# Norm chains of the second block kept apart by token half, with the first half's products ahead

## The chip, the core and the metric

The kernel runs on one core of a Trainium2 chip. TensorE (PE) multiplies; VectorE (DVE), ScalarE (ACT) and GpSimd (POOL) do the element-wise work; SyncE (SP) issues the weight loads. The metric is the time of one execution on the device in microseconds (us), taken as the median of several runs of one kernel.

## What is computed

Two blocks of a network work on 256 tokens of width 2048. The change lies in the second block, after its two output projections:

```python
x = x + rms_norm(o @ w_out[i], ln_mix_post[i])
h = rms_norm(x, ln_ffn_pre[i])
g, u = jnp.split(h @ w_gate_up[i], 2, axis=-1)
f = (jax.nn.silu(g) * u) @ w_down[i]
x = x + rms_norm(f, ln_ffn_post[i])
gate = jax.nn.sigmoid(rms_norm(x, ln_pli[i]) @ w_pli_gate[i])
x = x + gate * (p[i] @ w_pli_proj[i])
```

`rms_norm` divides each token's row of 2048 features by its root mean square, so the factor of a token is known only when the last column of its projection is there.

## The kernel before, in words

**Matrices.** Every fp32 product is made of three products of rounded parts: an operand is split into `hi` and `lo`, and hi·hi, hi·lo and lo·hi are added up in PSUM. Weights arrive as 256x512 pieces (`load`, line 354); each is split by ACT (`whi`, line 325) and DVE (`wlo`, line 326) into one of three ring buffers (`split`). `Block.steps` issues a unit of two k-tiles (k counts the 16 slices of 128 features) and all its matmuls stand on line 383. A unit of the projections (mode "tm") walks the two halves of the tokens, t = 0 and t = 1, and within each half its two k-tiles.

**Projections.** `project` (lines 1175 to 1200) runs the columns in groups (0, 1), (2), (3) of 512. When a group ends, ACT squares its PSUM tiles with a running sum (line 1188), DVE copies them to SBUF tiles `F[t, n]` (line 1205), and after group 2 the sums of the first three are put into `part`. Group 3's sum and copies are left to `post_norm`.

**The norm.** `post_norm` (lines 1207 to 1243) adds the last sum for both halves (1210), takes the power -1/2 on POOL (226), and builds for each half a diagonal matrix `dg` of its factors on ACT (1218). For k < 4 (`lead`) a product with `dg` on PE (1228, an fp32 matmul that the trace shows as two passes) scales and transposes in one; from k = 4 on, ACT scales `F` in place (1233) and PE transposes it (1234, one pass). For every k both halves land side by side in one PSUM buffer of the pool `pss`, which has three such buffers of 512 columns, one bank each; only 256 columns are used. DVE then adds the result to the residual `xr[k]` (1237), ACT and DVE split the scaled residual into `H[k]` (991, 992). After k = 5, 7, 9 and so on, one unit of the block that follows (`first`) is issued, four k-tiles behind. In the second norm, `x_rows` (1298, 1299) adds four transposes behind each unit.

**What follows.** `x_stats` squares the 16 tiles `xr` on ACT (929) and adds them up on DVE (930), while PE does two units of the block `second`; then PE needs the sum (`tok_sums`, line 240).

**Order.** PE's order is that of the program. The other engines are ordered by a scheduler at build time; `hot()` raises an operation over the weight splits. The order of every engine is then fixed, and each runs its queue in order.

Of the kernel before, what the change touches and what calls it, by code (L numbers as in the profile page):

```python
# [13 lines left out]
AF = mybir.ActivationFunctionType  # L14
ALU = mybir.AluOpType
# [4 lines left out]
P = 128  # L20
D = 2048
KT = D // P
L = 256
# [147 lines left out]
def kernel(ctx: ExitStack, tc: tile.TileContext, x, cx, vec, w_mod, w_in, ret_decay_f, ret_decay_b,  # L171
                           w_out, p_2, w_in_2, w_out_2, rel_bias, w_gate_up, w_down, w_pli_gate, w_pli_proj,
                           kca, kcr, kcb, out):
    nc = tc.nc
    out = out[0]
# [3 lines left out]
    def mk(pool, shape, tag, dt=F32, bufs=None):  # L179
        uid[0] += 1  # L180
        return pool.tile(shape, dt, tag=tag, name=f"{tag}_{uid[0]}", bufs=bufs)
# [15 lines left out]
    def side_ps():  # L197
        return mk(pss, [P, 512], "sd")
# [8 lines left out]
    def C(name, rows=P):  # L207
        a, b = CA[name]
        return ca[:rows, a:b]

    ident, ones = C("ident"), C("ones")
    V = {}
    for g, rows in enumerate(VEC_ROWS):
        o = g * P
# [5 lines left out]
    def hot():  # L220
        return tc.high_priority(offset=HOT)

    def rsq(v, n, tag="rq"):
        r = mk(sm, [P, n], tag)
        with hot():
            nc.gpsimd.tensor_tensor(out=r, in0=v, in1=C("nhalf")[:, :n], op=ALU.pow)
        return r

    def mean_eps(ps, n, width):
        v = mk(sm, [P, n], "mv")  # L230
        with hot():
            nc.vector.tensor_scalar(out=v, in0=ps, scalar1=1.0 / width, scalar2=EPS, op0=ALU.mult, op1=ALU.add)
        return v

    def tok_sums(accs):

        ps = side_ps()
        for a, acc in enumerate(accs):
            for t in range(2):
                nc.tensor.matmul(ps[:, 2 * a + t:2 * a + t + 1], lhsT=acc[:, t * P:(t + 1) * P],  # L240
                                 rhs=ones[:, 0:1], start=True, stop=True)
        return ps[:, :2 * len(accs)]
# [67 lines left out]
    for i in range(WB):  # L310
        for part in ("whi", "wlo"):
            mk(wsp, [P, 1024 + STEP // 4], f"{part}{i}", F32R)
            n = small.pop(0)
# [15 lines left out]
    class Block:  # L329
# [65 lines left out]
        def unit(self, kk):  # L395
            for _ in self.steps(kk):
                pass

        def run(self, korder):
            for a in range(0, len(korder), 2):  # L400
                self.unit(korder[a:a + 2])
            return self.ps
# [18 lines left out]
    xr = [None] * KT  # L421
# [4 lines left out]
    for s, src in enumerate((x, cx)):  # L426
        for a in range(2):
# [3 lines left out]
            for b in (0, 4):  # L431
                tc.keep_in_program_order(nc.sync.dma_start(out=xi[:, b:b + 4, :],
                                                           in_=src[:, 8 * a + b:8 * a + b + 4, :]))
# [530 lines left out]
    with hot():  # L964
        r = rsq(mean_eps(tok_sums(sqa), 4, D), 4)
# [22 lines left out]
    def scaled_split(dst, src, col):  # L988

        hi, lo = dst[:2]  # L990
        nc.scalar.activation(out=hi, in_=src, func=AF.Copy, scale=col)
        nc.vector.scalar_tensor_tensor(out=lo, in0=src, scalar=col, in1=hi, op0=ALU.mult, op1=ALU.subtract)

    def hl(pool, tag):
        return pair(pool, L, tag)
# [3 lines left out]
    ss8 = mk(hp, [P, 2, 4], "ss8")  # L999
    part = mk(hp, [P, 2], "part")  # L1000
# [154 lines left out]
    for g in range(2):  # L1155
        for kind, c0 in ((stick, 0), (dilated, 3072)):
# [10 lines left out]
            ps = Block(w_in_2, [(c0 + 2048 + 512 * g, 512)], mov, L, "tm", KT).run(ks)[0]  # L1167
# [5 lines left out]
    F = {}  # L1173

    def project(w, mov, korder, split_at):

        late = []
        for cbs in ((0, 1), (2,), (3,)):
            b = Block(w, [(cb_ * 512, 512) for cb_ in cbs], mov, L, "tm", len(korder))
            for a in range(0, len(korder), 2):  # L1180
                if cbs[0] == 0 and a == split_at:
                    sideq.drain()
                b.unit(korder[a:a + 2])
            for ci, cb_ in enumerate(cbs):
                for t in range(2):
                    jk = mk(tb, [P, 512], "tmp", BF16)
                    with hot():
                        nc.scalar.activation(out=jk, in_=b.ps[ci][t], func=AF.Square,
                                             accum_out=ss8[:, t, cb_:cb_ + 1])
                    for c_ in range(2):  # L1190
                        n = 2 * cb_ + c_
                        F[t, n] = mk(rp, [P, L], f"b{8 * t + n}")
                        late.append((F[t, n], b.ps[ci][t][:, c_ * L:(c_ + 1) * L]))
            if cbs[0] < 3:
                copies(late)
                late = []
            if cbs[0] == 2:
                nc.vector.tensor_reduce(out=part, in_=ss8[:, :, :3], axis=AX.X, op=ALU.add)
                nc.vector.tensor_scalar(out=part, in0=part, scalar1=1.0 / D, scalar2=EPS, op0=ALU.mult, op1=ALU.add)
        return late  # L1200

    def copies(todo):
        for f, ps in todo:
            with hot():
                nc.vector.tensor_copy(out=f, in_=ps)

    def post_norm(late, gain, next_gain, first, also=None):

        with hot():
            nc.vector.scalar_tensor_tensor(out=part, in0=ss8[:, :, 3], scalar=1.0 / D, in1=part, op0=ALU.mult,  # L1210
                                           op1=ALU.add)
        r = rsq(part, 2)
        copies(late)
        dg = []
        for t in range(2):
            d = mk(sm, [P, P], "dg")
            with hot():
                nc.scalar.activation(out=d, in_=ident, func=AF.Copy, scale=r[:, t:t + 1])
            dg.append(d)
        lead = 4  # L1220
        for k in range(KT + lead):
            if k < KT:
                ps = side_ps()
                for t in range(2):
                    f = F[t, k // 2]
                    o = (k % 2) * P
                    if k < lead:
                        nc.tensor.matmul(ps[:, t * P:(t + 1) * P], lhsT=f[:, o:o + P], rhs=dg[t],
                                         start=True, stop=True)
                        continue  # L1230
                    if k % 2 == 0:
                        with hot():
                            nc.scalar.activation(out=f, in_=f, func=AF.Copy, scale=r[:, t:t + 1])
                    nc.tensor.transpose(ps[:, t * P:(t + 1) * P], f[:, o:o + P], ident)  # L1234
                H[k] = hl(hp, f"h{k}")
                with hot():
                    nc.vector.scalar_tensor_tensor(out=xr[k], in0=ps[:, :L], scalar=V[gain][:, k:k + 1], in1=xr[k],
                                                   op0=ALU.mult, op1=ALU.add)
                    scaled_split(H[k], xr[k], V[next_gain][:, k:k + 1])
            if k % 2 and k > lead:  # L1240
                first.unit([k - lead - 1, k - lead])
                if also is not None:
                    also(k - lead - 1)

    def x_stats(b):

        for k in range(KT):
            sq_acc(xr[k], sqa[0], k == 0)
        b.run(ks[:4])
        m = mean_eps(tok_sums(sqa[:1]), 2, D)  # L1250
        b.run(ks[4:8])
        return rsq(m, 2)

    sideq.cap, sideq.rate = 4, 2
    late = project(w_out_2, lambda k: O[k], [0, 1, 2, 3, 8, 9, 10, 11, 4, 5, 6, 7, 12, 13, 14, 15], 12)
    def gate(j):
        return Block(w_gate_up, [(j * 512, 512)], mov, L, "fm", KT)

    def up(j):
        return Block(w_gate_up, [(DFF + j * 512, 512)], mov, L, "fm", KT)  # L1260

    first = gate(0)
    post_norm(late, "lpost", "lfpre", first)
    second = up(0)
    r = x_stats(second)
# [7 lines left out]
    for j in range(FT // 4):  # L1273
# [5 lines left out]
        ps = (second.ps if j == 0 else up(j).run(ks))[0]  # L1279
        for n in range(4):  # L1280
            f = 4 * j + n
            nc.vector.tensor_tensor(out=sgt[n], in0=ps[n][:, :L], in1=sgt[n], op=ALU.mult)
            nc.scalar.copy(out=G[f][0], in_=sgt[n])
            nc.vector.tensor_tensor(out=G[f][1], in0=sgt[n], in1=G[f][0], op=ALU.subtract)
    late = project(w_down, lambda k: G[k], list(range(FT)), -1)
    p4.close()
    p5 = ExitStack()
# [12 lines left out]

    first = Block(w_pli_gate, [(0, 512)], mov, L, "tm", KT)
    post_norm(late, "lfpost", "lpli", first, x_rows)
    second = Block(w_pli_gate, [(512, 512)], mov, L, "tm", KT)
    rp2 = x_stats(second)
# [47 lines left out]
```

## Time and profile before

| what | value |
|---|---|
| median of three runs | 2828.59 us (2826.74 to 2828.80) |
| the profiled execution, its time | 2829.03 us |
| span of the profiled execution | 2827.3 us |
| first norm, last projection matmul to first gate matmul | 1983.31 to 1989.44 us |
| second norm, the same | 2721.77 to 2727.44 us |

The profile is one execution. In its rows a group of instructions is given by start, duration, engine, line, tiles written and read, and in square brackets the idle time before it and what ended that time. "PE" rows are matmuls, "PEld" rows weight loads of TensorE.

### The profile page before, as it was taken

The numbers are of one execution on the slowest core, as the hardware profiler recorded it, in microseconds if no ns is written. First come the engines' busy times: TensorE is split into PE (matmuls) and PEld (weight loads), VectorE is DVE, ScalarE is ACT, GpSimd is POOL, SyncE is SP. The second block draws the span as 40 slices with busy tenths as digits, with TensorE's granted clock in tenths as the row PEclk, the third lists the DMA queues.
The fourth block names the chain that finished last, engine by engine and source line by source line (L and its number), as shares of the span: only waits on it lengthen the run. The fifth ranks groups of instructions, "written<-read, shape, count | busy, mean of one in ns | idle before, by whom it ended". The sixth has DMA issues, their size and how long they took to land.

```text
span 2827.3 us, 37469 instructions
## 1 busy us (share of the span) xinstructions
PE 2790.4 (99%) x14206; PEld 2345.9 (83%) x14206; DVE 1765.9 (62%) x2948; ACT 1227.4 (43%) x1964; POOL 82.6 (3%) x133
## 2 busy tenths in 40 slices
PE   7999999999999999999999999999999999999999
PEld 3588888888888878888888888888888888888878
DVE  4456765767586674745777765665766666654465
ACT  3323322422242253533556555554644544444464
POOL 0000000000000000100000010000000000000000
PEclk9999999999999999999999999999999999999999
DMA  9864454444465544646666665556556666666655
GB/s 370 299 181 137 141 164 153 145 146 143 163 207 168 169 156 156 210 142 185 210 201 214 200 202 171 165 167 191 163 188 193 188 192 188 192 193 193 208 177 168
DMA packets 159670, 522.80 MB, mean 185 GB/s; under 512 B 18232, under 2 KB 36928, under 8 KB 159232
## 3 DMA queue, kind: packets, MB, share of 16 engines
q1 hardware_dynamic: 155296, 508.78, 56.4%
q0 software_dynamic: 2752, 9.19, 1.2%
q8 instruction: 111, 1.82, 0.3%
q10 hardware_dynamic: 1440, 2.43, 0.2%
q14 instruction: 71, 0.58, 0.1%
HBM read 509.83 MB, written 7.88 MB: 183 GB/s over the span
## 4 chain that ended last, share of the span: by engine, by line
PE 96%; DMA 2%; DVE 1%; issue 0%; ACT 0%; SPq 0%; POOL 0%; DVEq 0%; ACTq 0%; POOLq 0%
PE mm L383 89%; PE sd L520 1%; DMA raw<-in_w_mod_dram 1%; PE sd L643 1%; PE sd L630 1%; PE sd L637 0%; PE sd L621 0%; DVE wlo L326 0%; PE sd L496 0%; PE sd L383 0%; DMA v<-in_ctx_dram 0%; DMA big<-in_w_mod_dram 0%; PE sd L1234 0%; PE sd L670 0%; DVE macc L489 0%
## 5 line engine op out<-in xcount | busy, mean ns | idle before, releaser
L326 DVE TENSOR_TENSOR wlo<-raw,whi 128x1024 fp32r<-128x1024 f32 (+1 forms) x764 | 916.3, 1200 | 796.7 <-ACT whi L325 794.1
L325 ACT CAST whi<-raw 128x1024 fp32r<-128x1024 f32 (+1 forms) x764 | 787.0, 1031 | 1289.9 <-PE mm L383 976.8
L383 PE MATMUL mm<-a,whi 128*128 128x512 f32 x3488 | 1134.7, 395 | 3.2 <-ACT a L558 1.6
L383 PEld LDWEIGHTS mm<-a,whi 128*128 128x128 f32 x3488 | 650.2, 188 | 160.4 <-issue 19.3
L383 PE MATMUL mm<-a,wlo 128*128 128x512 f32 (+1 forms) x2256 | 770.0, 341 | 0.0
L383 PE MATMUL mm<-h,whi 128*128 128x512 f32 x1920 | 670.9, 392 | 0.0
L383 PE MATMUL mm<-h,wlo 128*128 128x256 f32 x1920 | 541.2, 282 | 0.0
L383 PEld LDWEIGHTS mm<-a,wlo 128*128 128x128 f32 x2256 | 425.3, 189 | 49.6
L383 PEld LDWEIGHTS mm<-h,whi 128*128 128x128 f32 x1920 | 360.5, 188 | 75.2 <-issue 0.6
L383 PEld LDWEIGHTS mm<-h,wlo 128*128 128x128 f32 x1920 | 363.2, 189 | 0.0
L489 DVE SCALAR_TENSOR_TENSOR macc<-raw,s,macc 128x512 f32<-128x512 f32 x420 | 292.7, 744 | 59.8 <-DMA raw<-in_w_mod_dram 58.8
L383 PE MATMUL mm<-whi,f 128*128 128x512 f32 x704 | 216.8, 389 | 0.0
L383 PE MATMUL mm<-whi,h 128*128 128x512 f32 (+1 forms) x576 | 172.1, 373 | 0.0
L383 PE MATMUL mm<-whi,a 128*128 128x512 f32 x512 | 158.9, 390 | 0.0
L383 PEld LDWEIGHTS mm<-whi,f 128*128 128x128 f32 x704 | 132.1, 188 | 27.3
L383 PE MATMUL mm<-wlo,f 128*128 128x512 f32 x352 | 137.0, 389 | 0.0
L383 PEld LDWEIGHTS mm<-whi,h 128*128 128x128 f32 x576 | 104.3, 189 | 16.9
L383 PEld LDWEIGHTS mm<-whi,a 128*128 128x128 f32 x512 | 96.1, 188 | 19.9
L383 PE MATMUL mm<-wlo,h 128*128 128x512 f32 (+1 forms) x288 | 105.6, 367 | 0.0
L383 PE MATMUL mm<-wlo,a 128*128 128x512 f32 x256 | 99.7, 390 | 1.0 <-DVE wlo L326 1.0
L383 PE MATMUL mm<-whi,o 128*128 128x512 f32 x256 | 80.2, 391 | 0.0
L383 PEld LDWEIGHTS mm<-wlo,f 128*128 128x128 f32 x352 | 66.1, 188 | 13.8
(280 smaller groups left out, 2001.3 us busy)
## 6 DMA issues: line engine op xcount, KB each, us to landing
raw<-in_w_in_dram SPq DMA_DIRECT2D x344, 512.0 KB, 3.6
raw<-in_w_mod_dram SPq DMA_DIRECT2D x184, 512.0 KB, 4.3
raw<-in_w_gate_up_dram SPq DMA_DIRECT2D x176, 512.0 KB, 3.5
raw<-in_w_out_dram SPq DMA_DIRECT2D x96, 512.0 KB, 3.8
raw<-in_w_down_dram SPq DMA_DIRECT2D x88, 512.0 KB, 3.5
raw<-in_w_pli_gate_dram SPq DMA_DIRECT2D x24, 512.0 KB, 3.5
big<-in_w_mod_dram SPq DMA_DIRECT2D x8, 512.0 KB, 7.9
raw<-in_w_in_dram SPq DMA_DIRECT2D x16, 256.0 KB, 6.2
```

Of the source, the lines that this page charges most:

```text
L325: nc.scalar.copy(out=hi, in_=raw)
L326: nc.vector.tensor_tensor(out=lo, in0=raw, in1=hi, op=ALU.subtract)
L383: nc.tensor.matmul(o[b], lhsT=l_, rhs=r_, start=d0 + a == 0 and b == 0, stop=d0 + a == self.nk - 1 and b == len(tri) - 1)
L489: nc.vector.scalar_tensor_tensor(out=acc[v], in0=raw[:, a, :], scalar=sc, in1=acc[v], op0=ALU.mult, op1=ALU.add)
L520: nc.tensor.matmul(pr[32 * q:32 * q + 32, :], lhsT=s2w[:, 2 * k:2 * k + 32], rhs=raws[q // 2][:, q % 2, :], start=g == 0, stop=g == 3, til ...
L630: nc.tensor.matmul(ps[:, t * L:(t + 1) * L], lhsT=kT[:, q0 + t * P:q0 + (t + 1) * P], rhs=qT[:, q0:q0 + L], start=True, stop=True)
L643: nc.tensor.matmul(po[:, t * P:(t + 1) * P], lhsT=sc[:, jt * L + t * P:jt * L + (t + 1) * P], rhs=v[:, 2 * s + jt, :], start=(jt == 0), st ...
```

## The change

`project` no longer runs group 3's last two units as units. A new method `last` loads their two weight pieces and issues all 12 matmuls of half 0 over the last four k-tiles, then all 12 of half 1. `post_norm` makes the sum, the power, the copies and `dg` for each half by itself. The products with `dg` reach over k < 6, and all six of half 0 are issued ahead of half 1's. So that six results fit the three buffers of `pss`, two neighbouring k now share one buffer: even k takes its left 256 columns, odd k its right ones, for the later transposes too.

```diff
+        def last(self, kk):
+            col = self.cols[0]
+            whl = [self.load(kk[i:i + 2], col) for i in (0, 2)]
+            self.done += 4
+            for n in range(self.nt[0]):
+                s = slice(n * P, (n + 1) * P)
+                for i, k in enumerate(kk):
+                    xh, xl, xb = self.mov(k)
+                    hi, lo = (e[:, i % 2, :] for e in whl[i // 2])
+                    for b, (l_, r_) in enumerate([(xh, hi), (xh, lo), (xl, hi)]):
+                        nc.tensor.matmul(self.ps[0][n], lhsT=l_[:, s], rhs=r_, start=False, stop=i == 3 and b == 2)
...
+                if cbs[0] == 3 and a >= len(korder) - 4:
+                    if a == len(korder) - 4:
+                        b.last(korder[a:])
+                    continue
...
+        rs, dg = [], []
         for t in range(2):
+            c = part[:, t:t + 1]
+            with hot():
+                nc.vector.scalar_tensor_tensor(out=c, in0=ss8[:, t, 3:4], scalar=1.0 / D, in1=c, op0=ALU.mult,
+                                               op1=ALU.add)
+            rs.append(rsq(c, 1))
+            copies(late[2 * t:2 * t + 2])
             d = mk(sm, [P, P], "dg")
             with hot():
-                nc.scalar.activation(out=d, in_=ident, func=AF.Copy, scale=r[:, t:t + 1])
+                nc.scalar.activation(out=d, in_=ident, func=AF.Copy, scale=rs[t])
             dg.append(d)
-        lead = 4
+        lead = 6
+        tiles = {}
+        def scaled(k, t):
+            if k not in tiles:
+                ps = side_ps()
+                tiles[k], tiles[k + 1] = ps[:, :L], ps[:, L:]
+            o = (k % 2) * P
+            nc.tensor.matmul(tiles[k][:, t * P:(t + 1) * P], lhsT=F[t, k // 2][:, o:o + P], rhs=dg[t],
+                             start=True, stop=True)
+        for k in range(lead):
+            scaled(k, 0)
         for k in range(KT + lead):
             if k < KT:
...
+                if k < lead:
+                    scaled(k, 1)
+                else:
                     if k % 2 == 0:
+                        ps = side_ps()
+                        tiles[k], tiles[k + 1] = ps[:, :L], ps[:, L:]
+                    for t in range(2):
...
+                        nc.tensor.transpose(tiles[k][:, t * P:(t + 1) * P], f[:, o:o + P], ident)
...
-                    nc.vector.scalar_tensor_tensor(out=xr[k], in0=ps[:, :L], scalar=V[gain][:, k:k + 1], in1=xr[k],
+                    nc.vector.scalar_tensor_tensor(out=xr[k], in0=tiles[k], scalar=V[gain][:, k:k + 1], in1=xr[k],
```

## Rows read from the trace of the kernel before

**Rows 1.** The page: the chain that ended last, share of the span by engine.
```profile
PE 96%; DMA 2%; DVE 1%; issue 0%; ACT 0%; SPq 0%; POOL 0%; DVEq 0%; ACTq 0%; POOLq 0%
```

**Rows 2.** Timeline, first norm: start, duration, engine, line, operation [idle before, releaser].
```profile
1983.35 0.60 ACT L1188 ACTIVATE tmp<-mm 128x512 bf16<-128x512 f32 x1 [0.67 <-PE mm L383]
1983.84 0.19 ACT L1188 ACTIVATION_READ_ACCUMULATOR tmp<-mm 128x1 f32 x1
1984.07 0.16 DVE L1210 SCALAR_TENSOR_TENSOR part<-ss,part 128x2 f32<-128x2 f32 x1 [0.46 <-ACT tmp L1188]
1984.31 0.69 POOL L226 TENSOR_TENSOR rq<-part,ca 128x2 f32<-128x2 f32 x1 [81.13 <-DVE part L1210]
1985.00 1.22 DVE L326 TENSOR_TENSOR wlo<-raw,whi 128x1024 fp32r<-128x1024 f32 x1
1985.03 0.70 ACT L1218 ACTIVATE dg<-ca,rq 128x128 f32<-128x128 f32 x2
1985.49 3.50 PE L1228 MATMUL sd<-dg,b 128*128 128x128 f32 x16 [2.18 <-ACT dg L1218]
...
1989.44 0.48 PE L383 MATMUL mm<-h,whi 128*128 128x512 f32 x1
```

**Rows 3.** Timeline, second norm, the same columns.
```profile
2724.04 2.12 PE L1228 MATMUL sd<-dg,b 128*128 128x128 f32 x16 [2.27 <-ACT dg L1218]
...
2726.71 0.48 DVE L1237 SCALAR_TENSOR_TENSOR a<-sd,vecs,a 128x256 f32<-128x256 f32 x1
...
2727.25 0.44 PE L1234 MATMUL sd<-ca,b 128*128 128x128 f32 x2 [0.86 <-DVE a L1237]
...
2727.44 0.48 PE L383 MATMUL mm<-whi,h 128*128 128x512 f32 x1
```

**Rows 4.** Windows: stretch, length, busy us (instructions) by engine, granted clock, DMA share, GB/s.
```profile
1985.50:1988.60 3.10, 3.10 (x16) 3.10 (x17) 2.12 (x5) 2.79 (x7) 0.00 (x0) 0.58 0.45 132
...
2724.00:2726.00 2.00, 1.96 (x16) 1.96 (x17) 1.61 (x3) 2.00 (x6) 0.10 (x1) 1.00 0.61 168
...
1983.31:1989.44 6.13, 3.95 (x20) 3.95 (x21) 4.58 (x11) 5.64 (x13) 0.69 (x1) 0.72 0.55 171
...
2005.34:2019.81 14.47, 14.47 (x86) 12.62 (x84) 13.81 (x27) 10.95 (x24) 0.00 (x0) 1.00 0.62 179
```

**Rows 5.** Timeline, weight split in the projection's last unit; a copy of group 2.
```profile
1980.63 1.05 ACT L325 CAST whi<-raw 128x1024 fp32r<-128x1024 f32 x1 [1.67 <-PE mm L383]
...
1962.31 0.76 DVE L1205 COPY b<-mm 128x256 f32<-128x256 f32 x2 [0.47 <-ACT tmp L1188]
```

**Rows 6.** Line 1205 by itself: what ended its engine's idle time (us, times).
```profile
  ACT tmp L1188: 1.9, 4
```

**Rows 7.** Timeline, transposes of a pair of k and the two residual adds behind them.
```profile
1992.49 0.60 PE L1234 MATMUL sd<-ca,b 128*128 128x128 f32 x4
1992.91 0.88 DVE L1237 SCALAR_TENSOR_TENSOR a<-sd,vecs,a 128x256 f32<-128x256 f32 x2 [0.34 <-PE sd L1234]
1995.70 0.60 PE L1234 MATMUL sd<-ca,b 128*128 128x128 f32 x4
1996.86 0.87 DVE L1237 SCALAR_TENSOR_TENSOR a<-sd,vecs,a 128x256 f32<-128x256 f32 x2
...
2734.40 0.60 PE L1234 MATMUL sd<-ca,b 128*128 128x128 f32 x4
2735.29 0.88 DVE L1237 SCALAR_TENSOR_TENSOR a<-sd,vecs,a 128x256 f32<-128x256 f32 x2
```

**Rows 8.** The chain in order of time, a pair's transposes and a unit: start, us.
```profile
1992.65 0.44 PE sd L1234 x4
1993.09 2.78 PE mm L383 x16
```

**Rows 9.** Timeline of PE at the sum that `x_stats` makes, first norm.
```profile
2020.86 0.61 PE L240 MATMUL sd<-ca,sqa 128*128 128x1 f32 x4 [1.04 <-DVE sqa L930]
```

More of the change, by code (lines that the diff above doesn't have):

```diff
@@ L1207, in post_norm @@
     def post_norm(late, gain, next_gain, first, also=None):
[L1209 to L1214, printed above, removed]
-        for t in range(2):
+        rs, dg = [], []
+        for t in range(2):
+            c = part[:, t:t + 1]
[4 more added lines that the diff above has]
+            copies(late[2 * t:2 * t + 2])
@@ L1221, in post_norm @@
+        for k in range(lead):
+            scaled(k, 0)
         for k in range(KT + lead):
             if k < KT:
[L1223 to L1230, printed above, removed]
-                    if k % 2 == 0:
-                        with hot():
-                            nc.scalar.activation(out=f, in_=f, func=AF.Copy, scale=r[:, t:t + 1])
-                    nc.tensor.transpose(ps[:, t * P:(t + 1) * P], f[:, o:o + P], ident)
+                if k < lead:
+                    scaled(k, 1)
+                else:
+                    if k % 2 == 0:
+                        ps = side_ps()
+                        tiles[k], tiles[k + 1] = ps[:, :L], ps[:, L:]
+                    for t in range(2):
+                        f = F[t, k // 2]
+                        o = (k % 2) * P
+                        if k % 2 == 0:
+                            with hot():
+                                nc.scalar.activation(out=f, in_=f, func=AF.Copy, scale=rs[t])
+                        nc.tensor.transpose(tiles[k][:, t * P:(t + 1) * P], f[:, o:o + P], ident)
```

## The prediction

> **What bounds the kernel now.** I began with the chain of waits on the page: PE makes up 96% of it [rows 1]. So only what moves PE's last matmul counts, and the change can win at most the time in which PE stands idle or crawls around the two norms. The timeline of each norm came next. In the first, PE ends the projection at 1985.49 - 2.18 = 1983.31 us and stands for 2.18 us, because the chain square, sum, power, `dg` runs by itself: 0.60 and 0.19 on ACT, 0.16 on DVE, 0.69 on POOL, half of 0.70 on ACT, with short gaps between [rows 2]. Then come 16 passes of the products with `dg` and two pairs of transposes, and the first gate matmul starts at 1989.44, 6.13 us after the projection's end [rows 2]. In the second norm the idle time is 2.27 us and the way to the first gate matmul 2727.44 - (2724.04 - 2.27) = 5.67 us [rows 3]. About 2.6 us of each of these is necessary PE work (2.12 for 16 passes, 0.44 for four transposes [rows 3, 8]), so what could be won is some 3.5 + 3.1 us in all, 0.23% of the time. The windows show two more things: the first norm's products ran at a granted clock of 0.58, mostly the 1.2 GHz level, after 2.18 us without work, while the second's kept 1.00, 2.4 GHz, after 2.27 us [rows 4]. And DVE is nearly full behind the first norm, 13.81 of 14.47 us [rows 4], until PE waits 1.04 us for DVE's sum [rows 9].
>
> **The change, part by part.** Let T be the end of the last projection matmul. It stays where it is: 24 matmuls are reordered, none is added. The weights of the last two units are now read by both halves, so the older ring buffer comes free about half a unit later, 1.4 us (a unit lasts 2.78 [rows 8]). The weight split that started at 1980.63, one unit before T [rows 5], starts near T - 1.3; its parts take 1.05 and 1.22 us [rows 2, 5]. What is queued behind it is the second half's sum on DVE and `dg` on ACT. The split's DVE part would end near T + 1.0, where the second half's square is done at T + 0.76, so 0 to 0.3 us is lost there. The weight loads follow their buffers; SP issues as many as before, and the gate's next two units are split already, so nobody waits for them.
>
> The first half's chain starts a unit's length earlier, at T - 2.7, and needs 2.2 us; half 1's matmuls hide all of it. Its 12 passes (six k, two passes each, 2.12/16 = 0.13 us a pass [rows 3]) run from T to T + 1.6 where PE stood idle. The second power on POOL (0.69) and second sum (0.16) lie on the second half's chain as the single ones did. That chain cannot begin before T, so half 1's products start at T + 2.2 to T + 2.5; I take P = T + 2.4. Up to here some 1.6 us of PE work per norm has moved into idle time: that is the gain.
>
> Now the price. Even and odd k share a PSUM bank. Odd k's product, a write by PE, stands in PE's queue behind even k's, and even k's residual add on DVE reads that same bank in between. The trace of before has no PE write beside a DVE read of one bank. The nearest row: DVE's copy of a projection tile at 1962.31 waited 0.47 us for ACT's square of the same tile, though both only read it; four copies did so, 1.9 us in all [rows 5, 6]. Two readers need no order for the data's sake, so the bank itself is handed over from engine to engine. A write and a read will be treated no better. From below, the wait is nothing, if disjoint columns are let through (first rival); from above, a full hand-over for each pair. I take the hand-over, since its row is two engines at one bank.
>
> The Trainium skill speaks against the change here too: PSUM — Partial Sum Buffer, "PSUM bank collisions raise a hardware error", states that two engines at one bank and quadrant collide even at different addresses, and wants a guard by bank and not by address. By its rule the hand-over is certain and the time the forecast's; by a guard on columns alone, the first rival's. No run here shows the error.
>
> A hand-over costs, from even k's product to odd k's: 0.42 us until DVE starts (1992.49 to 1992.91 [rows 7]), 0.48 for the add, and 0.06 until PE goes on (2726.71 + 0.48 to 2727.25 [rows 3]), together 0.96. In the head six k go by and then the transposes of k = 6 and 7, whose odd half waits likewise; only then comes the first gate unit, where before it came behind k = 5, in separate buffers. From one odd k to the next it takes 0.42 + 0.40 (the second of two adds, 0.88 - 0.48 [rows 3, 7]) + 0.48 + 0.06 = 1.36. So: 0.96 + 3 x 1.36 + 0.22 (two transposes, half of 0.44 [rows 8]) = 5.26 us from P to the first gate matmul if DVE does nothing else. The halves `lo` of the same k also want DVE; each gap of 1.36 - 0.88 = 0.48 us holds one of the two, so 0 to 1.2 us more. First gate matmul: T + 7.5 to T + 9.0, say T + 8.2. Against 6.13 and 5.67 that is +1.3 to +2.9 (2.1) and +1.8 to +3.3 (2.5). One pair of transposes more is then done than before, -0.44 each [rows 8]: 1.6 and 2.1 us in the middle.
>
> Behind the head, before, a pair of transposes took 0.44 us and PE went straight into its unit [rows 8]. After, four pairs per norm (8, 9 to 14, 15) wait between even and odd: 0.42 + 0.48 + 0.06 - 0.22 = 0.74 us, plus what DVE is late. It was 0, 0.74 and 0.47 us late at the pairs shown (1992.91, 1996.86 and 2735.29 against 0.42 behind their transposes [rows 7]). PE's new waits give DVE room, so I take 0.3 and keep 0 to 0.74: 1.04 a pair, 4.2 us a norm (3.0 to 5.9).
>
> One thing comes back: in the first norm PE waited 1.04 us for DVE's sum [rows 9]; a late PE finds it ready. DVE is full there, but it gains as much time as PE loses, so the sum does not come later than PE.
>
> **Sum.** First norm 1.6 + 4.2 - 1.0 = 4.8 us (2.8 to 7.3); second 2.1 + 4.2 = 6.3 (4.4 to 8.8). The clock: PE has 7 to 8 thin microseconds in each head, and one of two heads before lost 3.50 - 2.12 = 1.38 us to a lower clock [rows 2, 3]. My steps are at full clock, so I add half of it, 0.7 (0 to 2.8 for both). Together 11.8 us (7.2 to 18.9). The profiled execution takes 2829.03, so 2840.8; it lies 0.44 above the median of the runs, so the median after is 2840.3, +0.41%. A difference under 0.2%, 5.7 us, is about what a measurement of this kernel cannot tell from none.
>
> **The rivals.**
>
> *No hand-over (not slower).* If odd k's product may be written while even k is read, half 1's products run through: six k in 1.6 us, transposes 0.44, first gate unit at P + 2.0 to 2.4, T + 4.6. That is 1.5 and 1.1 us earlier than before and 0.44 each for the transposes: 1.9 and 1.5. In the first norm DVE decides: it is nearly full up to the sum that PE waits for, so it gives back at most what it idled in the head, 6.13 - 4.58 = 1.55 us [rows 4], say 0.8. Result -2.3 us, 2826.3. It decides from the point where the first odd product starts before the first add ends. For it: the columns are disjoint. Against it: the four copies that waited for a mere reader [rows 6].
>
> *Hand-over, but half hidden.* If DVE takes every even add at once, `lo` never comes between, and later slack of PE takes up some, the cost is about 4 us: 2832.6. Against it: PE runs in order and stands elsewhere in this part only for the 1.04 us already counted.
>
> *The clock falls in both norms and stays low into the first units.* Another 2 us or more on the forecast: 2843 to 2847. For it: the first norm's 0.58; against it: the second's 1.00 after an equal gap [rows 4].
>
> *The change does not do what it says:* if the late weight split stands ahead of `dg` of half 0 on ACT, its products begin up to 1 us after T and push half 1's by about 0.4 us. That adds under 1 us in all and stays within the forecast.
>
> **How the numbers follow.** Forecast with hand-over 0.64, clock rival 0.12, no hand-over 0.12, half hidden 0.07, unforeseen gain 0.05. Slower by over 0.2%: 0.64 + 0.12 = 0.76. Within: 0.12 + 0.07 = 0.19. Faster: 0.05. By its bounds without the clock's upper end the forecast spans 2835.8 to 2844.7; with the half hidden case below and the clock above the range is 2831 to 2849, which leaves out the no-hand-over case and little more.
>
> **What would show it.** Right: PE rows of line 1234 (its new number) in twos, not fours, with idle time before the second two that ends on the residual add; products of half 1 likewise for odd k; first gate matmul some 8 us behind the last projection matmul; no wait at the sum of the first norm. Wrong: half 1's 12 passes in one piece of 1.6 us, and the first gate matmul under 5 us behind the projection. The part on the first half is right if its 12 passes start within 0.3 us of T. I would be wrong above all if the scheduler lets PE and DVE work on the two halves of a bank at once.

## The result and the profile after

The changed kernel takes 2845.93 us (median of four runs, 2844.59 to 2847.73) against 2828.43 before: a ratio of 1.0064, 95% interval 1.0052 to 1.0076. It is 17.5 us slower. The profiled execution spans 2844.0 us against 2827.3.

Its line numbers are moved: the square is on 1205, the copies on 1222, the sum on 1230, `dg` on 1236, the products with `dg` on 1247, the scaling in place on 1265, the transposes on 1266, the residual add on 1269, and `last`'s matmuls on 410.

The list of waits on PE shows what is new. Its columns are: engine and line that waited, what it waited for, us in total, times, longest.

```profile
PE sd L1266 <- DVE a L1269: 7.5, 10, 1.9
PE sd L1247 <- ACT dg L1236: 4.5, 2, 3.1
PE sd L1247 <- DVE a L1269: 4.3, 6, 1.1
```

Sixteen times PE stood at a product or transpose until a residual add of DVE was done: 6 products and 10 transposes, one for each odd k of the two norms. Before, this engine pair made one wait, 0.86 us [rows 3], and of another kind: each k had a buffer, and k = 5 waited for k = 2's to come free. The wait for `dg` is as long in sum as before (4.5 us against 2.18 + 2.27 [rows 2, 3]), though half of the products no longer wait for it.

The timeline of the first norm, the columns of [rows 2]:

```profile
1980.05 1.69 ACT L1265 ACTIVATE b<-b,rq 128x256 f32<-128x256 f32 x4
1980.49 0.40 PE L410 MATMUL mm<-whi,o 128*128 128x512 f32 x1
1980.73 1.50 PE L1247 MATMUL sd<-dg,b 128*128 128x128 f32 x12
1981.65 0.57 ACT L1205 ACTIVATE tmp<-mm 128x512 bf16<-128x512 f32 x1
1983.63 0.49 PE L1247 MATMUL sd<-dg,b 128*128 128x128 f32 x2 [1.40 <-ACT dg L1236]
1984.16 0.48 DVE L1269 SCALAR_TENSOR_TENSOR a<-sd,vecs,a 128x256 f32<-128x256 f32 x1 [0.98 <-PE sd L1247]
1984.70 0.71 PE L1247 MATMUL sd<-dg,b 128*128 128x128 f32 x4 [0.58 <-DVE a L1269]
...
1988.02 1.23 DVE L326 TENSOR_TENSOR wlo<-raw,whi 128x1024 fp32r<-128x1024 f32 x1
1988.32 0.63 PE L1266 MATMUL sd<-ca,b 128*128 128x128 f32 x2
1989.16 0.48 DVE L1269 SCALAR_TENSOR_TENSOR a<-sd,vecs,a 128x256 f32<-128x256 f32 x1
1990.34 0.48 DVE L1269 SCALAR_TENSOR_TENSOR a<-sd,vecs,a 128x256 f32<-128x256 f32 x1
1990.88 0.69 PE L1266 MATMUL sd<-ca,b 128*128 128x128 f32 x2 [1.93 <-DVE a L1269]
1991.22 0.78 PE L383 MATMUL mm<-h,whi 128*128 128x512 f32 x1
...
1996.49 0.50 PE L1266 MATMUL sd<-ca,b 128*128 128x128 f32 x2
1997.56 0.45 PE L1266 MATMUL sd<-ca,b 128*128 128x128 f32 x2 [0.58 <-DVE a L1269]
...
2026.56 0.50 PE L240 MATMUL sd<-ca,sqa 128*128 128x1 f32 x4
```

The projection ends at T = 1980.49 + 0.40 = 1980.89. The 12 passes of half 0 follow without a gap. Half 1's products start at T + 2.74. Then PE goes in steps: two passes, a wait for the add, four passes, a wait. The first gate matmul comes at T + 10.33; before it was 6.13 [rows 2]. The first gate unit lasts from 1991.22 to 1996.49, 5.27 us, where one took 2.78 [rows 8]. The windows say why (stretch, length, busy us and instructions by engine, granted clock, DMA share, GB/s):

```profile
1988.89:1990.89 2.00, 0.07 (x2) 0.01 (x1) 2.00 (x6) 2.00 (x5) 0.00 (x0) 0.50 0.31 35
1990.89:1992.89 2.00, 2.00 (x7) 1.81 (x8) 2.00 (x4) 0.99 (x4) 0.00 (x0) 0.50 0.59 227
1992.89:1994.89 2.00, 2.00 (x7) 1.71 (x7) 1.31 (x4) 0.82 (x2) 0.00 (x0) 0.50 0.77 160
1994.89:1996.89 2.00, 2.00 (x8) 1.54 (x7) 0.00 (x0) 0.38 (x1) 0.00 (x0) 0.54 0.25 102
```

The granted clock is 0.50, the 1.2 GHz level, from the thin end of the head through the whole first unit. In the second norm the same happens, and the start of half 1 is later:

```profile
2726.89 1.69 ACT L1265 ACTIVATE b<-b,rq 128x256 f32<-128x256 f32 x4
2726.98 0.39 PE L410 MATMUL mm<-whi,f 128*128 128x512 f32 x1
2728.48 0.58 ACT L1205 ACTIVATE tmp<-mm 128x512 bf16<-128x512 f32 x1
2729.45 1.98 ACT L325 CAST whi<-raw 128x1024 fp32r<-128x1024 f32 x2
2731.33 0.40 ACT L1236 ACTIVATE dg<-ca,rq 128x128 f32<-128x128 f32 x1
2731.79 0.49 PE L1247 MATMUL sd<-dg,b 128*128 128x128 f32 x2 [3.08 <-ACT dg L1236]
2739.09 0.78 PE L383 MATMUL mm<-whi,h 128*128 128x512 f32 x1
...
2744.31 0.60 PE L1330 MATMUL sd<-ca,a 128*128 128x128 f32 x4
...
2777.56 0.50 PE L240 MATMUL sd<-ca,sqa 128*128 128x1 f32 x4
```

T is 2727.37 here; half 1's products start at T + 4.42, the first gate matmul at T + 11.72 (5.67 before [rows 3]), and its unit takes 2744.31 - 2739.09 = 5.22 us, again at the lower clock:

```profile
2739.09:2744.31 5.22, 5.22 (x15) 4.00 (x14) 3.55 (x9) 2.33 (x6) 0.00 (x0) 0.51 0.01 2
```

I measure each norm from T to the sum that `x_stats` makes (line 240), where PE's thin stretch is over. Before: 2020.86 - 1983.31 = 37.55 us in the first norm [rows 2, 9]; in the second the sum stood at 2760.92, 39.15 us behind the projection's end:

```profile
2760.92 0.50 PE L240 MATMUL sd<-ca,sqa 128*128 128x1 f32 x4
```

After: 45.67 and 50.19 us, so the norms cost 8.1 + 11.0 = 19.1 us more. The span grew by 16.7: the part ahead of the first norm happened to be 2.4 us shorter in this execution (T at 1980.89 against 1983.31). That is scatter; in the profiles of the experiments below the first T lies between 1980.3 and 1986.2 us, and two executions of kernels that differ only behind it are 5.7 us apart there.

| us from T | before, norm 1 | after, norm 1 | before, norm 2 | after, norm 2 |
|---|---|---|---|---|
| products of half 1 | 2.18 | 2.74 | 2.27 | 4.42 |
| first gate matmul | 6.13 | 10.33 | 5.67 | 11.72 |
| sum of `x_stats` | 37.55 | 45.67 | 39.15 | 50.19 |

### The profile page after: what moved, and what is told of

It reads as the page before. It is cut to its first block, busy times and chain, and to the rows that moved or that the text cites. A ratio compares the mean times of both kernels' runs of the same rounds, so it can differ in the third digit from the quotient of the medians.

```text
span 2844.0 us, 37484 instructions
## 1 busy us (share of the span) xinstructions
PE 2797.9 (98%) x14214; PEld 2349.2 (83%) x14214; DVE 1766.0 (62%) x2950; ACT 1228.3 (43%) x1960; POOL 86.0 (3%) x135
## 4 chain that ended last, share of the span: by engine, by line
PE 52%; DVE 1%; ACT 0%; issue 0%; DMA 0%; POOL 0%; ACTq 0%; DVEq 0%; POOLq 0%
PE mm L383 49%; DVE a L1269 0%; PE sd L1266 0%; DVE wlo L326 0%; PE mm L410 0%; ACT whi L325 0%; PE sd L656 0%; PE sd L1330 0%; PE sd L1096 0%; PE sd L650 0%; PE sd L1131 0%; PE sd L643 0%; PE sd L634 0%; PE sd L1112 0%; DMA raw<-in_w_in_dram 0%
```

## The experiments

The theory is that of the prediction: what costs is the hand-over of one PSUM bank from PE to DVE and back for each odd k. The main rival is that the chain per half costs, with the late weight split that `last` brings and the longer queues on ACT. The ratios below are against runs of the kernel before on the same chip.

**Sharing alone, put into the kernel before** (`share`):

```diff
-                ps = side_ps()
+                if k % 2 == 0:
+                    both = side_ps()
+                ps = both[:, (k % 2) * L:(k % 2 + 1) * L]
```

> The kernel before, with one edit: two neighbouring k share one PSUM buffer. Theory (sharing a bank costs): five pairs behind the head wait 0.74 us each per norm, 7.4 us, the head grows by 0.5 to 1.0 us, the first norm's 1.04 us comes back, and where the clock falls in the first gate unit 2.4 us per norm come on top: 2835 to 2842. Rival (chain per half costs): 2828, no change.

Measured: 2842.55 us, ratio 1.0057 (1.0044 to 1.0069), 15.4 us above the kernel before on that chip and 0.5 above the expected range: its first gate matmuls came 2.2 and 3.4 us later than before (T + 8.31 and 9.04), not 0.5 to 1.0. Its waits on PE:

```profile
PE sd L1236 <- DVE a L1239: 7.8, 12, 0.9
PE sd L1230 <- ACT dg L1218: 4.5, 2, 2.3
PE sd L1230 <- DVE a L1239: 2.3, 4, 0.6
```

Sixteen waits between odd product and even add again, in a kernel with one joint chain, no `last` and no product ahead. One edit brings nearly the whole loss of the change.

**Sharing, but both k written before either is read** (`share_pairs`). The kernel before, where even k's turn in the loop issues both k's products or transposes:

```diff
-                ps = side_ps()
-                for t in range(2):
-                    f = F[t, k // 2]
...
+                if k % 2 == 0:
+                    both = side_ps()
+                    for kk in (k, k + 1):
+                        ps = both[:, (kk % 2) * L:(kk % 2 + 1) * L]
+                        for t in range(2):
+                            f = F[t, kk // 2]
...
+                ps = both[:, (k % 2) * L:(k % 2 + 1) * L]
```

> The kernel before with two neighbouring k in one PSUM buffer, as in the run that shared the buffer alone and took 2842.6 us, but PE issues the products or transposes of both k before the first residual add. Theory (the price is the hand-over of the bank between PE's write of one k and DVE's read of the other, not the sharing): 2825 to 2830, no wait between the two k. Rival (sharing itself costs, since three buffers then turn over in pairs): 2835 to 2843.

Measured: 2829.43 us, ratio 1.0007 (0.9998 to 1.0015). The bank is shared as in `share`; only PE's order differs, and the waits on the adds are gone from the list:

```profile
PE sd L1231 <- ACT dg L1218: 4.4, 2, 2.3
PE sd L240 <- DVE sqa L930: 1.3, 1, 1.3
```

So three buffers that turn over in pairs cost nothing that can be measured. What costs is a write of PE queued between two reads of the same bank. `share` and `share_pairs` together settle that. They leave open why PE has to wait: the wait is one of the program's own semaphores, and a buffer of `pss` is one bank, so it may go by buffer or by bank. It does not go by columns. What the chip would do without it, no run here shows.

**The changed kernel with the same order** (`pairs`) and **with a buffer for each k** (`own`). In `pairs` the products and transposes of k and k + 1 are issued before the first add:

```diff
+                if k % 2 == 0:
+                    put(k)
+                    put(k + 1)
```

> The changed kernel, but PE issues both k of a bank before DVE's first add of that bank; banks are still shared, six products of half 0 still ahead. Theory (the bank is handed over between PE and DVE for every odd k, and the lower clock follows from that idling): the 8 waits of line 1266 and 6 of 1247 on the residual add go, PE's granted clock stays near 1.00 in the first gate unit, first gate matmul at 5 to 7 us behind the projection instead of 10.3 and 11.7; time 2827 to 2831. Rival (the chain per half, with its late weight split and two powers, is what costs): the waits may go but the time stays above 2838.

In `own` every k takes its own buffer, so half 0 runs ahead for three k and the units follow four k behind:

```diff
-        lead = 6
+        lead = 4
...
-                tiles[k], tiles[k + 1] = ps[:, :L], ps[:, L:]
+                tiles[k] = side_ps()[:, :L]
...
-        for k in range(lead):
+        for k in range(3):
             scaled(k, 0)
```

> The changed kernel, but each k has a PSUM buffer of its own; three buffers, so half 0's products run ahead for k < 3 only and units follow four k behind as before. Theory (sharing a bank costs): 2825 to 2830, no wait between even and odd k. Rival (chain per half costs): above 2838.

Measured: `pairs` 2830.42 us, ratio 1.0011 (1.0002 to 1.0020); `own` 2830.20 us, 1.0014 (1.0005 to 1.0023). By losing the hand-overs both take back about 14 of the change's 17.5 us; in `pairs` no wait on an add over 0.2 us is left around the norms (there were 6 and 10, not the 6 and 8 of its expectation). Against the theory, both still lie a little above the kernel before, `own` 0.2 above its range. The profile of `own` in its second norm shows what is left:

```profile
2718.22 1.69 ACT L1264 ACTIVATE b<-b,rq 128x256 f32<-128x256 f32 x4
...
2719.82 0.57 ACT L1205 ACTIVATE tmp<-mm 128x512 bf16<-128x512 f32 x1
...
2721.19 1.98 ACT L325 CAST whi<-raw 128x1024 fp32r<-128x1024 f32 x2
...
2723.07 0.40 ACT L1236 ACTIVATE dg<-ca,rq 128x128 f32<-128x128 f32 x1
...
2723.52 2.76 PE L1246 MATMUL sd<-dg,b 128*128 128x128 f32 x10 [4.17 <-ACT dg L1236]
```

T is 2718.68. Half 0's scalings in place (four, 1.69 us), which nobody needs yet, stand on ACT ahead of half 1's square, which starts 1.14 us late. Two weight splits then stand ahead of half 1's `dg`. Half 1's products start at T + 4.84, where the joint chain took 2.27. In `pairs` the scalings push a weight split too: in its first norm ACT's part of it comes only at T + 6.2 (at T - 0.8 in `pairs_late`, below), the second gate unit waits for DVE's part, and the clock falls there.

```profile
1994.73 0.58 PE L383 MATMUL mm<-h,wlo 128*128 128x256 f32 x1 [2.26 <-DVE wlo L326]
```

**The scalings held back** (`pairs_late`, `own_late`). The second power covers both halves, and the scalings take their factors from it:

```diff
-            rs.append(rsq(c, 1))
+            rs.append(rsq(part[:, :t + 1], t + 1))
...
-                                nc.scalar.activation(out=f, in_=f, func=AF.Copy, scale=rs[t])
+                                nc.scalar.activation(out=f, in_=f, func=AF.Copy, scale=rs[1][:, t:t + 1])
```

> The kernel that issues both k of a bank before the first add, with one more edit: ACT's scaling in place of half 0 takes its factors from the second power, so it cannot stand ahead of half 1's square on ACT. In the run without the edit four scalings (1.7 us) did, and half 1's square started 1.1 us behind the projection's end in the second norm. Theory (this queue on ACT is what kept the chain per half from winning): half 1's products start 2.2 to 2.6 us behind the projection in both norms instead of 2.7 and 4.4, time 1 to 4 us below the run without the edit, 2824 to 2828. Rival (DVE is the bound behind the head): products earlier, time within 1 us of the run without the edit.

> The kernel with a buffer of its own for each k, with the same edit on the scaling. Theory: half 1's products at 2.2 to 2.6 us in both norms instead of 2.7 and 4.8; time 1 to 4 us lower, 2824 to 2828, at or below the kernel before. Rival (DVE is the bound): within 1 us.

Measured: `pairs_late` 2824.20 us, ratio 0.9993 (0.9984 to 1.0002); `own_late` 2828.53 us, 1.0006 (0.9997 to 1.0015). Measured against the kernel before on each chip, the first gained 5 to 6 us on `pairs`, more than expected; the second gained 1 to 2 us on `own`, and it missed the expected range by 0.5. (In its first norm the clock fell during the products of half 1, as in the kernel before.) Half 1's products start 2.79 and 3.25 us behind T in `pairs_late`, not at 2.2 to 2.6:

```profile
1981.51 1.23 DVE L326 TENSOR_TENSOR wlo<-raw,whi 128x1024 fp32r<-128x1024 f32 x1 [1.37 <-ACT whi L325]
1982.65 0.15 DVE L1230 SCALAR_TENSOR_TENSOR part<-ss,part 128x1 f32<-128x1 f32 x1
...
1984.08 1.60 PE L1247 MATMUL sd<-dg,b 128*128 128x128 f32 x12 [1.46 <-ACT dg L1236]
1985.85 0.63 PE L1266 MATMUL sd<-ca,b 128*128 128x128 f32 x4 [0.17 <-DVE a L1275]
```

T is 1981.29. The late weight split ends on DVE at 1982.74, and half 1's sum goes behind it. From there on all 12 passes of half 1 run in one piece of 1.6 us, and the clock stays at 1.00 through both heads. From T to the sum of `x_stats`: 35.30 and 38.68 us, 2.3 and 0.5 less than before.

The gain on `pairs` is therefore only in part what the theory said. From T to the sum `pairs` took 39.32 and 40.84 us. In its first norm half 1's products started at T + 2.74 already, so none of the 4.0 us there comes from an earlier start; what is gone is the wait of 2.26 us for the weight split and the fall of the clock at it. In the second norm the start moved from 4.41 to 3.25, and the clock, which had fallen in `pairs`, stayed up.

> The same kernel as pairs_late once more, beside the others on one chip. Expected 0.5 to 4 us below the kernel before; a median at or above it would say that its lead of 2.4 us was scatter.

Measured: 2825.53 us, ratio 0.9995 (0.9986 to 1.0004); 35.29 and 38.66 us in its profile. The two norms repeat to 0.02 us, while the runs scatter by 6 us; neither interval alone excludes no change.

**Half 0 not ahead** (`own_late_joint`), the two products of each k one behind the other:

```diff
-        for k in range(3):
-            scaled(k, 0)
...
-                    if k >= 3:
-                        scaled(k, 0)
+                    scaled(k, 0)
```

> As own_late, but half 0's products are not ahead: each k has its two products one behind the other, as in the kernel before; the chain per half and the late units stay. Theory: six passes per norm (0.8 us) move out of idle time again, 0.5 to 2 us slower than own_late. Rival (what is ahead is hidden by DVE): no difference.

Measured: 2828.87 us, 0.3 above `own_late`, ratio 1.0006 (0.9997 to 1.0015), the same as that one's. The profiles put 0.3 and 0.6 us between the two from T to the sum. Their sum is within what was expected, but too little for the runs to tell from the rival's no difference; and in the second norm the clock fell in `own_late_joint` and not in `own_late`. With three products ahead, then, having them ahead is worth 1 us at most by these rows, and that is not shown by the times.

**`last` undone** (`nolast`), in the changed kernel:

```diff
-                if cbs[0] == 3 and a >= len(korder) - 4:
-                    if a == len(korder) - 4:
-                        b.last(korder[a:])
-                    continue
```

> The changed kernel, but the last two units of the projection run as units again; banks shared, six products ahead. Theory (sharing a bank is nearly all of the loss): half 0's chain ends some 1.4 us later, still within the idle time; 2843 to 2848. Rival (the late weight split that comes with the joined units costs): 2830 to 2838.

Measured: 2845.74 us, ratio 1.0067 (1.0054 to 1.0079), the time of the changed kernel. From T to the sum it takes 44.70 and 50.42 us, 1.0 less and 0.2 more than the changed kernel. `last` and its late weight split are no part of the loss that the runs can tell; the rival falls.

**`last` undone without the hand-over** (`pl_units`): `pairs_late` with the edit of `nolast`.

> pairs_late, but the last two units of the projection run as units again, so the weight split is no longer late. In pairs_late that split (1.22 us on DVE) held half 1's sum back by 0.5 us. Theory (the late split costs what it holds back): half 1's products 0.4 to 0.6 us earlier in each norm, half 0's products start 0.8 us behind the projection's end and still end before them; 0 to 1.2 us below pairs_late. Rival (half 0's products now push half 1's): equal or up to 1 us slower.

Measured: 2824.50 us, ratio 0.9990 (0.9981 to 0.9999), the one version whose interval lies below 1: 2.7 us faster than the kernel before on that chip. From T to the sum it takes 35.30 and 38.66 us, together 2.7 less than before, so the gain is where the change wanted it. It beats the changed kernel clearly and the kernel before narrowly, but not as I expected: half 1's products still start 2.80 and 3.24 us behind T. ACT's rows of the first norm say why:

```profile
1980.86 0.40 ACT L1232 ACTIVATE dg<-ca,rq 128x128 f32<-128x128 f32 x1 [1.00 <-POOL rq L226]
1981.16 0.58 ACT L1201 ACTIVATE tmp<-mm 128x512 bf16<-128x512 f32 x1
```

T is 1980.50. Half 0's `dg`, which waits for POOL, stands ahead of half 1's square; without `last` half 0 is half a unit later, so ACT's queue now loses what DVE's lost. It lies 1.0 us below `pairs_late` on the same chip, but both take the same time in the two norms to 0.01 us, so that difference is scatter.

**Units four behind** (`pl_lag4`): `pl_units` with the first gate unit ahead of the transposes of k = 6 and 7.

```diff
+        lag = 4
-        for k in range(KT + lead):
+        for k in range(KT + lag):
...
-            if k % 2 and k > lead:
-                first.unit([k - lead - 1, k - lead])
+            if k % 2 and k > lag:
+                first.unit([k - lag - 1, k - lag])
```

> pl_units with the units four k behind the transposes instead of six, so the first gate unit comes ahead of the transposes of k = 6 and 7. Theory (PE is the bound in the head): first gate matmul 0.4 to 0.8 us earlier, but the same transposes are done later, so within 0.5 us of pl_units. Rival (DVE is late with the halves that the first unit reads): a wait before the first unit, 0 to 2 us slower.

Measured: 2825.47 us, ratio 0.9992 (0.9983 to 1.0001). The first gate matmul stands at T + 5.65 and 5.26 against 5.66 and 5.40 in `pl_units`, though four transposes are fewer ahead of it; the sum comes 0.5 us later in each norm. The rival is nearer: the first unit waits for the halves, 1.25 us on DVE in the first norm and 0.39 on ACT in the second. The difference of the times cannot be told from none.

**PE kept busy** (`busy`): the changed kernel with products of two constants that nobody reads.

```diff
+        spare = main_ps()
+        def busy(n):
+            for _ in range(n):
+                nc.tensor.matmul(spare[:, :P], lhsT=ident, rhs=ident, start=True, stop=True)
...
+        busy(5)
...
+                if k % 2 and k < 8:
+                    busy(3 if k == 7 else 2)
```

> The changed kernel with extra products that nobody reads, put on PE where it waits (5 behind half 0's products, 2 or 3 ahead of odd k up to 7): the hand-overs stay, PE's idle time in the head is filled. Theory (idle PE lets the clock fall to 1.2 GHz, and the first gate unit then takes 5.2 us instead of 2.8): clock near 1.00 in the first unit, 2839 to 2842. Rival (the clock falls for another reason, or its price is hidden by DVE): 2845 to 2848.

Measured: 2845.75 us, ratio 1.0067 (1.0055 to 1.0080), in the rival's range. Two windows of its first norm, from 10 us behind T:

```profile
1993.71:1995.71 2.00, 0.67 (x6) 0.48 (x4) 2.00 (x6) 0.80 (x2) 0.00 (x0) 0.75 0.55 125
1995.71:1997.71 2.00, 2.00 (x8) 1.71 (x7) 1.97 (x6) 1.27 (x5) 0.00 (x0) 0.50 0.46 182
```

There the clock stayed at 1.00 for 11 us instead of 5.6, but fell all the same ahead of the first unit, and the head grew from 10.33 to 11.95 us. The second norm came out otherwise. The clock fell 5.0 us behind T, earlier than in the changed kernel, and was back at 1.00 when the first gate unit began:

```profile
2742.58:2745.42 2.84, 2.84 (x15) 2.30 (x14) 2.70 (x8) 1.80 (x6) 0.00 (x0) 1.00 0.03 6
...
2742.59 0.48 PE L383 MATMUL mm<-whi,h 128*128 128x512 f32 x1
...
2745.43 0.60 PE L1339 MATMUL sd<-ca,a 128*128 128x128 f32 x4
...
2778.69 0.50 PE L240 MATMUL sd<-ca,sqa 128*128 128x1 f32 x4
```

This unit takes 2745.43 - 2742.59 = 2.84 us, against 5.22 in the changed kernel, and the four pairs behind it wait 0.58 us each as they did there. From the first gate matmul to the sum it is 36.10 us, against 2777.56 - 2739.09 = 38.47: the 2.4 us that the unit gains all arrive at the sum. So this is what the clock cost the second norm there, and DVE does not hide it. The edit failed to hold the clock up in the head, so it gives no price for that part; what it saves is too little for the times to show.

## Why the prediction was right

**The sign and the mechanism** held: slower, by the hand-over of a shared bank. The nearest row from which I took it, DVE's copy that waited for ACT's square [rows 5, 6], had the right meaning: at least 0.58 us of PE's wait for each even add, 0.96 us from even to odd product (2000.62 to 2001.58, say), as computed from [rows 3, 7]. The waits on disjoint columns agree with what the Trainium skill states in PSUM — Partial Sum Buffer, "PSUM bank collisions raise a hardware error", a guard by bank and not by address; its figures on the error are shown by no run here.

```profile
2000.62 0.38 PE L1266 MATMUL sd<-ca,b 128*128 128x128 f32 x2
2001.58 0.44 PE L1266 MATMUL sd<-ca,b 128*128 128x128 f32 x2 [0.58 <-DVE a L1269]
```

**The size** was forecast at 11.8 us and measured at 17.5. The 2845.93 us lie in the range of 2831 to 2849, but 1.2 us above the span that the forecast itself was given (2835.8 to 2844.7), in the window of the clock rival (2843 to 2847), which had a chance of 0.12. Term by term:

- Half 0's products: said from T to T + 1.6, found in one piece of 1.50 us straight behind the projection in both norms. Right.
- Half 1's products: said T + 2.4, found 2.74 and 4.42. I had one weight split in the queues, started near T - 1.3, ahead of half 1's sum and `dg`; in the first norm none stood there. I had not seen that half 0's early factors also release four scalings (1.69 us), which go ahead of half 1's square, nor two splits together ahead of `dg` (1.98 us) in the second norm. Term too small by 0.3 and 2.0 us.
- From there to the first gate matmul: said 5.3 to 6.5, found 7.59 and 7.30. In the first norm a weight split on DVE (1.23 us at 1988.02) went ahead of the add that k = 7 waits for, 1.93 us of wait there; in the second the first add stood behind two splits on DVE (2.36 us from 2730.52), and the later part of the stretch ran at the lower clock.
- The four pairs behind the head: said 1.04 us each (0.74 to 1.48), found 0.74, the lower bound, at nearly all of them (0.96 less 0.22). DVE was late at none; only the first took 1.07, its transposes still at the lower clock. Too large by 1.2 us a norm.
- The clock: said 0.7 us in all, bound 2.8. The first unit alone lost 5.27 - 2.78 = 2.5 and 5.22 - 2.78 = 2.4 us. This is the term that was furthest off. I priced a head at the lower clock, but not a full unit behind it; only the rival did. The second norm of `busy` bears out the price: 2.4 us.
- The sum in the first norm: the 1.04 us came back, no wait of PE on line 240 is left. Right.

Added up for the first norm: 10.33 - 6.13 - 0.44 (one pair of transposes more) = 3.8 for the head, 2.5 for the clock, 3.0 for the pairs, less 1.0: 8.3, against 8.1 measured. For the second: 11.72 - 5.67 - 0.44 = 5.6, 2.4 and 3.0: 11.0, as measured. Heads and clock were put too low and the pairs too high, so the total is nearer than its terms.

**What the runs showed in place of my picture of the change:** once PE writes both k of a bank before DVE reads, and the scalings are kept from going ahead, the chain per half comes out 2.7 us below the kernel before (`pl_units`), and 4.9 us below `share_pairs`, which has the joint chain in that order, on the same chip. By the rows from T to the sum it is 2.7 and 1.9 us; of the 2.7, 3.50 - 2.12 = 1.4 us are the clock that fell in the first norm before [rows 2, 3]. In `share_pairs` itself there is no gain; in `pairs`, with the scalings ahead, none either. `pl_units` also has six products with `dg` in place of four, which no run parts from the rest.

What stays open: how much of the 15 us that `share` costs is the waits and how much the clock that falls behind them. Its first units took 4.22 and 5.17 us against 2.94 and 2.86 (the first norm of `pairs`, the second of the kernel before), so an estimate for the clock in them is 3.6 us; what it cost in the heads is not parted from the waits.

## What to carry to other kernels

When a PSUM buffer is packed with two results, issue all of PE's writes to it before the first read of another engine: one order cost 0.57%, the other nothing that the runs can tell. When a chain is split so that its first half starts early, look at everything that the early result releases on an in-order engine, since work that nobody waits for may take the place of the second half's first step, or of a weight split that the next unit needs. And price a stall of PE with the unit behind it at the lower clock, not with the stall alone.

## What the runs showed of the hardware that I had not expected

The granted clock cannot be told from the length of one idle stretch. It fell to the 1.2 GHz level after 2.18 us without work in the first norm before, stayed at 1.00 after 2.27 us in the second [rows 4], stayed at 1.00 after 2.07 us in the first norm of `own`, and fell in its second after 4.17. The same stretch, 2.57 us ahead of half 1's products, left it at 1.00 in the second norm of `own_late`, and it fell in the first of `own_late_joint`. In `share_pairs`, `pairs_late` and `pl_units` it stayed at 1.00 through both heads; in the changed kernel, `share` and `nolast`, whose heads are cut into many short waits, it fell in every norm, for some 7 to 10 us, and in the first norm of the changed kernel before any stretch longer than 1.40 us. In `pairs` it fell in both norms with no wait on an add, once around the 2.26 us for a weight split, once after 3.07 us without work.
